# Ranking the experts on the chip and giving ScalarE and VectorE 64 slots for experts with few tokens, in a two-layer GLA/SSD trunk with a top-2-of-8 mixture of experts

## The chip, the cores and the metric

The kernel runs on one core of one Trainium2 chip. The metric is the device time of one execution in microseconds (us), and the time of a kernel is the median of several executions. Engines are named as the profile names them: PE (TensorE matmul), PEld (TensorE weight load), DVE (VectorE), ACT (ScalarE), POOL (GpSimd), SP (SyncE, which here issues the DMAs of the weights).

## The reference

Two layers work on 256 tokens of width 1024. Each layer is a mixer (gated linear attention beside a Mamba-2 scan) and a feed-forward part; the first layer has a dense SwiGLU, the second a mixture of 8 experts, of which each token uses 2:

```python
D_MODEL = 1024; SEQ = 256; D_FF = 3584; N_EXPERTS = 8; TOP_K = 2

def swiglu(t, w_gate, w_up, w_down):
    return (jax.nn.silu(t @ w_gate) * (t @ w_up)) @ w_down

def moe_swiglu(h, router_w, w_gate, w_up, w_down):
    t = h.reshape(bsz * seq, d)
    logits = (t @ router_w).astype(jnp.float32)
    top_v, top_i = lax.top_k(logits, TOP_K)
    top_p = jax.nn.softmax(top_v, axis=-1)
    gates = jnp.sum(jax.nn.one_hot(top_i, N_EXPERTS) * top_p[..., None], axis=1)
    out = jnp.zeros_like(t)
    for e in range(N_EXPERTS):
        out = out + gates[:, e:e + 1] * swiglu(t, w_gate[e], w_up[e], w_down[e])
    return out.reshape(bsz, seq, d)
```

256 tokens with 2 experts each make 512 pairs, 64 per expert on average. All data is float32.

## The kernel before

**Items.** The change touches the mixture of experts, which is the last and longest stage. The weights of an expert (3 matrices of 1024 x 3584) are cut into 42 pieces of 1 MiB, called items here. `moe_order` yields them: the hidden width is cut into 7 chunks `c` of 512, and each chunk has two items of gate weights (G), two of up weights (U) and two of down weights (D, one chunk behind). `moe_items` puts them on a plan, in the order of the experts 0 to 7.

**From memory to PE.** `pump` lets SP issue the DMA of the next planned item (L154) as soon as one of the staging buffers (`raw` twice, `xm`, `xx`, `q`, `xce`, `ada`, and `acc` in the first expert) is free. `split_whole` turns an item into two float32r halves, since PE multiplies in that format: ACT copies the high half (L182, 128x2048) and DVE subtracts it from the item (L183, 128x2048), after which the staging buffer is free. The halves go to `ws` slots, ten in all and two per item, and PE frees them.

**Slots.** Of the tokens an expert gets at most 128 at a time; `slot_map` (L1498) builds the matrix that gathers them, `gather` (L1512) gathers, and `split_cols` (L482, L495, L496) cuts the gathered tokens into high and low halves. `few` says of each expert whether it has at most 64 tokens. `is_narrow` (L1600) loads that into a register of PE, and `modal` (L1195) makes PE branch on it. With at most 64 tokens, high and low half of a token stand side by side as 128 columns, and an item costs PE 8 matmuls of 512 columns in place of 12 (`mm_slots`, L1205 and L1211 in place of L1207, L1208 and L1211); `folded` (L1256) then adds the two halves of each result, in place of a plain transpose (L1258). An expert with at most 64 tokens is called narrow below, another one wide.

**A chunk on ACT and DVE.** When gate and up products of a chunk are done, `run_experts` queues five steps, some items apart: `copy` (ACT, L1247, `gs` and `us`), `gate` (fold on PE, then SiLU on ACT, L1271), `hidden` (fold on PE, then a product on DVE, L1275), and `parted` (ACT copy L1280 and DVE subtraction L1281, which make the halves `fth` that the down product uses). All of these work on 128x512, that is 4 blocks of 128 slots, whether the expert is narrow or wide. Each engine works in the order in which its instructions are written.

**The next expert.** `at` places the rest by expert, chunk and item: at chunk 3 the slot map of the next expert, at chunk 4 its gather and split, and in chunks 1 and 2 the `combine` (L1560) of the expert before, which adds its output to `acc`. `make_gates` runs in expert 0, chunk 1.

Of the kernel before, what the change touches and what calls it, by code (L numbers as in the profile page):

```python
# [50 lines left out]
def trunk(ctx: ExitStack, tc: tile.TileContext, a: dict, out: bass.AP):  # L51
# [79 lines left out]
    def pump():  # L131
        n = len(raws)
        while n < len(extra) and state["dma"] < len(plan):
# [8 lines left out]
            elif kind == "adah":  # L142
                l, j, hf, k = what
                c0 = j * D + hf * 512
                view = a["ada_w"][l, k * 512:(k + 1) * 512, c0:c0 + 512].rearrange("(k p) n -> p k n", p=P)
            else:
                view = what
# [1090 lines left out]
    def run_experts(mo, experts, operand, fold, at):  # L1238
# [11 lines left out]
        def folded(src, narrow, p):  # L1250

            def body(nar):
                for k in range(4):
                    ks = slice(k * P, (k + 1) * P)
                    if nar:
                        pe.matmul(p[:, ks], src[:, ks], fold, start=True, stop=True)  # L1256
                    else:
                        pe.transpose(p[:, ks], src[:, ks], ident)  # L1258

            modal(narrow, body)  # L1260
            return p
# [7 lines left out]
        def gate(key):  # L1269
            sil[key] = mo.tile([P, FC], F, name=nm("fsg"), tag="fsg")  # L1270
            act.activation(sil[key], folded(gs.pop(key), ops[key[0]][1], ps_t()), AF.Silu)  # L1271

        def hidden(key):
            p, s = folded(us.pop(key), ops[key[0]][1], ps_mm()), sil[key]
            dve.tensor_tensor(s, p, s, op=OP.mult)  # L1275

        def parted(key):
            t = th[key] = mo.tile([P, 4, P, 2], R, name=nm("fth"), tag="fth", bufs=2)
            sv = sil.pop(key).rearrange("p (k t) -> p k t", k=4)
            act.activation(t[:, :, :, 0], sv, AF.Copy)  # L1280
            dve.tensor_tensor(t[:, :, :, 1], sv, t[:, :, :, 0].bitcast(F), op=OP.subtract)  # L1281

        for n, (kind, e, c, i) in enumerate(order):
# [3 lines left out]
            X, narrow = ops[e]  # L1287
# [58 lines left out]
    def moe_items(experts):  # L1346
        wg, wu, wd = a["moe_w_gate"][0], a["moe_w_up"][0], a["moe_w_down"][0]
        for kind, e, c, i in moe_order(experts):
            f0 = c * FC
            if kind in "GU":  # L1350
                w = (wg if kind == "G" else wu)[e, i * 512:(i + 1) * 512, f0:f0 + FC]
                w_item(w.rearrange("(k p) n -> p k n", p=P), [4, FC])
            elif kind == "D":
                w_item(wd[e, f0 + i * 256:f0 + (i + 1) * 256, :].rearrange("(k p) n -> p k n", p=P), [2, D])
            else:
                w_item(wd[e, f0:f0 + FC, i * 512:(i + 1) * 512].rearrange("(k p) n -> p k n", p=P), [4, 512])


    def moe(mo, ys, row, mT):
# [30 lines left out]
        few = mo.tile([P, NE], I32, name="few")  # L1390

# [98 lines left out]

        def slot_map(e, base):

            pm = pm_
            if base:
                sl = mo.tile([P, 2], F, name=nm("sl"), tag="sl", bufs=2)
                dve.tensor_scalar(sl, pos[:, :, e], float(-base), None, op0=OP.add)
            for t in range(2):
                dve.tensor_scalar(pm[:, t], iota_s, sl[:, t:t + 1] if base else pos[:, t, e:e + 1], mr[:, t, e:e + 1],  # L1498
# [3 lines left out]
        def pairs(e):  # L1502

            for t in range(2):
                dve.tensor_scalar(pm2[:, t], iota_h, pos[:, t, e:e + 1], mr[:, t, e:e + 1], op0=OP.is_equal, op1=OP.mult)
# [41 lines left out]
        def combine(e, pT, yhl, hf, first, dst, ps=ps_mm):  # L1547
            hs = slice(hf * 512, (hf + 1) * 512)
            for t in range(2):
# [6 lines left out]
                g = gates[:, t, e:e + 1]  # L1556
# [42 lines left out]
        def is_narrow(e):  # L1599
            return pe.value_load(few[0:1, e:e + 1], min_val=0, max_val=1)  # L1600
# [7 lines left out]

        def at(e, c, t, ys):
            nonlocal acc, fnw  # L1610
            where = (c, t)
            if e == 0:
                if where == (0, 1):
                    pT[0] = slots_T(0, pm, free, narrow[0])
                if where == (1, 1):
                    make_gates()
                if where == (0, 3):
# [14 lines left out]
            if e < NE - 1:  # L1632
# [4 lines left out]
                if where == (4, 1):  # L1637
                    split_cols(*gathered(e + 1, 0), *gather(m["pm"], 0, free))
                if where == (4, 3):
                    pT[e + 1] = slots_T(e + 1, m["pm"], free, narrow[e + 1])  # L1640
                if where == (4, 5):
                    split_cols(*gathered(e + 1, 1), *gather(m["pm"], 1, free))
# [12 lines left out]
        y = run_experts(mo, list(range(NE)), lambda e: (xg[e % 2], narrow[e]), fold, at)  # L1655
# [12 lines left out]
        with tc.If(over > 0):  # L1668
            xg.clear()
# [140 lines left out]
```

## Time and profile before

| | |
|---|---|
| median of three executions | 1522.16 us (1520.71 to 1522.85) |
| the profiled execution | 1522.08 us, its span 1520.3 us |
| first matmul of expert 0 | 570.0 us into the span |
| last matmul of the last expert | about 1508 us into the span |
| DVE, PE, ACT busy share of the span | 86%, 92%, 70% |
| read from memory | 480 MB, of it 352 MB for the experts |

The profile's span is 1.8 us shorter than the execution's own time, because some work lies around it. A busy share is an average over stages of different kinds; the stage of the experts has to be read alone, and there expert by expert. [...] The DMA share is the time of all packets over that of 16 engines, and can pass 1.

### The profile page before, as it was taken

The page shows a single profiled execution, that of the slowest core. Times are in us where ns is not written, and L with a number is a line of the kernel's source. Part 1 is how long each engine was busy: PE and PEld are TensorE (multiplying, and loading weights), DVE is VectorE, ACT ScalarE, POOL GpSimd, SP SyncE. Part 2 cuts the span into 40 slices and gives each one's busy share as a digit, 9 for nine tenths or more (in the row PEclk, how much of TensorE's full clock was granted, in tenths as well). Part 3 has the DMA queues.
Part 4 walks back from the last instruction along what each step waited for, and adds up shares of the span by engine and source line. Part 5 has one row for each costly group of instructions (what it writes and reads, how often), then busy time and mean ns, then how long its engine had stood idle before and what let it go on. Part 6 is the DMA issues. An engine that isn't in the chain of part 4 may idle for free.

```text
span 1520.3 us, 20693 instructions
## 1 busy us (share of the span) xinstructions
PE 1406.2 (92%) x7578; PEld 1203.3 (79%) x7578; DVE 1309.5 (86%) x1170; ACT 1069.5 (70%) x1258; POOL 41.5 (3%) x68
## 2 busy tenths in 40 slices
PE   4998899999999896999999899999899999999986
PEld 3886699999889785878888777777778888888764
DVE  7888878777757658999889999999999888888996
ACT  3474545444548457898778889898887777778875
POOL 2011000000010100000000000000000000000001
PEclk9999999999999988999999999999999999999988
DMA  9974688888844445999999999999999999999992
GB/s 335 311 249 158 230 279 318 314 321 308 298 148 146 140 165 205 380 379 398 375 320 371 389 398 402 404 402 402 406 403 400 381 325 351 346 321 376 384 375 96
DMA packets 204603, 483.15 MB, mean 318 GB/s; under 512 B 13119, under 2 KB 15405, under 8 KB 204462
## 3 DMA queue, kind: packets, MB, share of 16 engines
q1 hardware_dynamic: 203890, 480.05, 85.9%
q8 instruction: 98, 1.61, 0.4%
q10 hardware_dynamic: 428, 0.63, 0.1%
q0 software_dynamic: 144, 0.52, 0.1%
q14 instruction: 43, 0.35, 0.1%
HBM read 480.12 MB, written 1.05 MB: 316 GB/s over the span
## 4 chain that ended last, share of the span: by engine, by line
PE 44%; DVE 7%; issue 4%; ACT 4%; DMA 2%; POOL 0%; DVEq 0%; ACTq 0%
PE mm L1211 9%; DVE ws L183 5%; PE y L1211 5%; PE mm L1207 5%; PE mm L1208 5%; PE mm L1205 4%; PE y L1205 3%; PE y L1207 3%; PE y L1208 3%; ACT ws L182 2%; PE pt L1256 2%; PE y L1512 1%; PE mm L1256 1%; DMA raw<-in_moe_w_down 1%; DMA xm<-in_moe_w_down 1%
## 5 line engine op out<-in xcount | busy, mean ns | idle before, releaser
L174 ACT ACTIVATE ws<-raw 128x1024 fp32r<-128x1024 f32 x136 | 143.8, 1061 | 136.9 <-PE mm L428 64.1
L183 DVE TENSOR_TENSOR ws<-raw,ws 128x2048 fp32r<-128x2048 f32 x97 | 221.5, 2285 | 18.7 <-ACT ws L182 17.8
L175 DVE TENSOR_TENSOR ws<-raw,ws 128x1024 fp32r<-128x1024 f32 x136 | 164.3, 1221 | 56.5 <-ACT ws L174 55.9
L182 ACT ACTIVATE ws<-raw 128x2048 fp32r<-128x2048 f32 x97 | 185.8, 1916 | 32.0 <-PE y L1208 9.4
L1211 PE MATMUL y<-ws,fth 128*128 128x512 f32 x448 | 126.1, 404 | 0.0
L1211 PE MATMUL mm<-ws,hTh 128*128 128x512 f32 x448 | 122.1, 395 | 0.0
L1211 PE MATMUL mm<-ws,hTl 128*128 128x512 f32 x448 | 121.7, 393 | 0.0
L365 DVE SCALAR_TENSOR_TENSOR ada<-raw,s_col,ada 128x1024 f32<-128x1024 f32 (+1 forms) x98 | 114.3, 1167 | 2.1
L183 DVE TENSOR_TENSOR ws<-xx,ws 128x2048 fp32r<-128x2048 f32 x47 | 107.4, 2285 | 7.5 <-ACT ws L182 7.3
L183 DVE TENSOR_TENSOR ws<-ada,ws 128x2048 fp32r<-128x2048 f32 x47 | 107.4, 2285 | 7.3 <-ACT ws L182 7.3
L183 DVE TENSOR_TENSOR ws<-xm,ws 128x2048 fp32r<-128x2048 f32 x46 | 105.2, 2287 | 9.6 <-ACT ws L182 9.5
L183 DVE TENSOR_TENSOR ws<-xce,ws 128x2048 fp32r<-128x2048 f32 x47 | 107.3, 2284 | 6.8 <-ACT ws L182 6.8
L183 DVE TENSOR_TENSOR ws<-q,ws 128x2048 fp32r<-128x2048 f32 x47 | 107.3, 2284 | 5.4 <-ACT ws L182 4.8
L426 PE MATMUL mm<-hTh,ws 128*128 128x256 f32 x384 | 107.9, 281 | 0.0
L427 PE MATMUL mm<-hTh,ws 128*128 128x256 f32 x384 | 106.8, 278 | 0.0
L428 PE MATMUL mm<-hTl,ws 128*128 128x256 f32 x384 | 106.7, 278 | 0.0
L1211 PEld LDWEIGHTS y<-ws,fth 128*128 128x128 f32 x448 | 89.1, 199 | 19.9
L182 ACT ACTIVATE ws<-q 128x2048 fp32r<-128x2048 f32 x47 | 90.1, 1918 | 15.2 <-PE mm L1208 5.0
L182 ACT ACTIVATE ws<-ada 128x2048 fp32r<-128x2048 f32 x47 | 90.2, 1918 | 14.5 <-PE mm L1208 5.7
L1211 PEld LDWEIGHTS mm<-ws,hTh 128*128 128x128 f32 x448 | 85.5, 191 | 18.7
L1211 PEld LDWEIGHTS mm<-ws,hTl 128*128 128x128 f32 x448 | 85.8, 191 | 18.0
L182 ACT ACTIVATE ws<-xce 128x2048 fp32r<-128x2048 f32 x47 | 90.3, 1922 | 12.2 <-PE mm L1208 6.6
(378 smaller groups left out, 3451.1 us busy)
## 6 DMA issues: line engine op xcount, KB each, us to landing
raw<-in_ada_w SPq DMA_DIRECT2D x48, 1024.0 KB, 6.0
raw<-in_moe_w_up SPq DMA_DIRECT2D x33, 1024.0 KB, 6.6
raw<-in_moe_w_gate SPq DMA_DIRECT2D x32, 1024.0 KB, 7.8
raw<-in_moe_w_down SPq DMA_DIRECT2D x32, 1024.0 KB, 8.9
raw<-in_w_in SPq DMA_DIRECT2D x21, 1024.0 KB, 5.3
ada<-in_moe_w_down SPq DMA_DIRECT2D x17, 1024.0 KB, 8.8
xx<-in_moe_w_gate SPq DMA_DIRECT2D x16, 1024.0 KB, 7.5
q<-in_moe_w_gate SPq DMA_DIRECT2D x16, 1024.0 KB, 7.5
```

Of the source, the lines that this page charges most:

```text
L174: act.activation(h, src, AF.Copy)
L175: dve.tensor_tensor(lo, src, h.bitcast(F), op=OP.subtract)
L182: act.activation(h, r, AF.Copy)
L183: low = lambda: dve.tensor_tensor(lo, r, h.bitcast(F), op=OP.subtract)
L365: dve.scalar_tensor_tensor(acc, w, s_col[:, k:k + 1], acc, op0=OP.mult, op1=OP.add)
L426: pe.matmul(ps, xh, wh, start=start, stop=False)
L427: pe.matmul(ps, xl, wh, start=False, stop=False)
L428: pe.matmul(ps, xh, wl, start=False, stop=stop)
L1205: pe.matmul(ps, xs[:, 0:HALF].rearrange("p s two -> p (s two)"), wh, start=start, stop=False)
L1207: pe.matmul(ps, xs[:, :, 0], wh, start=start, stop=False)
L1208: pe.matmul(ps, xs[:, :, 1], wh, start=False, stop=False)
L1211: pe.matmul(ps, both if nar else xs[:, :, 0], wl, start=False, stop=stop)
```

## The change

The first expert stays expert 0. For the other seven the chip computes a rank by token count, and works on them in turns: the one with the most tokens, the one with the fewest, the second most, the second fewest and so on. The rank is made in expert 0 at chunk 1, item 3 (`arrange`, 18 instructions on DVE), and `order` then holds each expert's columns in the new order. SP loads the seven numbers into registers, and the DMAs of experts 1 to 7 take the expert from the register, which adds one register instruction to each of 294 DMAs. `is_narrow` loads its flag into registers of PE, ACT and DVE, and `modal` now also encloses the steps of ACT and DVE: in a narrow expert SiLU, `hidden`, `parted` and `split_cols` work on 4 blocks of 64 slots in place of 128.

```diff
+        def blocks(t, nar):
+            return t.rearrange("p (k t) -> p k t", k=4)[:, :, :HALF if nar else P]
...
         def hidden(key):
-            p, s = folded(us.pop(key), ops[key[0]][1], ps_mm()), sil[key]
-            dve.tensor_tensor(s, p, s, op=OP.mult)
+            src, p, s = us.pop(key), ps_mm(), sil[key]
+
+            def body(nar):
+                folded(src, nar, p)
+                sv = blocks(s, nar)
+                dve.tensor_tensor(sv, blocks(p, nar), sv, op=OP.mult)
+
+            modal(ops[key[0]][2], body)
...
+            def body(nar):
+                sv, tv = blocks(s, nar), t[:, :, :HALF if nar else P]
+                act.activation(tv[:, :, :, 0], sv, AF.Copy)
+                dve.tensor_tensor(tv[:, :, :, 1], sv, tv[:, :, :, 0].bitcast(F), op=OP.subtract)
...
+            def view():
+                return w[bass.ds(index(e), 1), r, n].rearrange("o (k p) n -> p (o k) n", p=P)
...
+        def arrange():
...
+            dve.scalar_tensor_tensor(key, cnt, float(NE), iota_e, op0=OP.mult, op1=OP.add)
+            dve.memset(key[:, 0:1], -1.0)
+            dve.tensor_tensor(pick, key[:, None, :].to_broadcast([P, NE, NE]),
+                              key[:, :, None].to_broadcast([P, NE, NE]), op=OP.is_lt)
+            dve.tensor_reduce(key, pick, axis=AX.X, op=OP.add)
...
+            dve.tensor_tensor(picked, pick[:, None].to_broadcast([P, 8, NE, NE]),
+                              info[:, :, None, :].to_broadcast([P, 8, NE, NE]), op=OP.mult)
+            dve.tensor_reduce(order, picked, axis=AX.X, op=OP.add)
...
         def is_narrow(e):
-            return pe.value_load(few[0:1, e:e + 1], min_val=0, max_val=1)
+            f = ids[0:1, 0, e:e + 1] if e else few[0:1, 0:1]
+            return pe.value_load(f, min_val=0, max_val=1), nc.values_load(
+                f, engines=[mybir.EngineType.PE, mybir.EngineType.Activation, mybir.EngineType.DVE], min_val=0, max_val=1)
...
+                if where == (1, 3):
+                    arrange()
+                    arranged[0] = True
+                    for i in range(1, NE):
+                        place[i] = sp.value_load(ids[0:1, 1, i:i + 1], min_val=0, max_val=NE - 1)
...
-                    split_cols(*gathered(e + 1, 0), *gather(m["pm"], 0, free))
+                    split_slots(e + 1, 0)
```

On DVE, in the middle of expert 2, a chunk's two own steps stand between the subtractions L183 of the items. Before:

```order
L183 TENSOR_TENSOR ws_8989<-xce_8748,ws_8988 128x2048
L1195 UNCONDITIONAL_BRANCH x2
L1275 TENSOR_TENSOR fsg_8921<-mm_8994,fsg_8921 128x512
L495 CAST hTl_5976<-sct_9014 128x512
L496 TENSOR_TENSOR hTl_5976<-sct_9014,hTl_5976 128x512
L183 TENSOR_TENSOR ws_9044<-raw_1169_8775,ws_9043 128x2048
L1195 UNCONDITIONAL_BRANCH
L1281 TENSOR_TENSOR fth_9049<-fsg_8921,fth_9049 128x512
L183 TENSOR_TENSOR ws_9074<-ada_8814,ws_9073 128x2048
```

The same two steps on DVE in the changed kernel, `hidden` (now L1285) and `parted` (now L1296), one chunk earlier, where no split of the next expert falls between them:

```order
L183 TENSOR_TENSOR ws_8803<-ada_8564,ws_8802 128x2048
L1195 COMPARE_AND_BRANCH
L1285 TENSOR_TENSOR fsg_8742<-mm_8808,fsg_8742 128x4x64
L1195 UNCONDITIONAL_BRANCH
L1285 TENSOR_TENSOR fsg_8742<-mm_8808,fsg_8742 128x512
L1195 UNCONDITIONAL_BRANCH x2
L183 TENSOR_TENSOR ws_8843<-raw_1120_8599,ws_8842 128x2048
L1195 COMPARE_AND_BRANCH
L1296 TENSOR_TENSOR fth_8848<-fsg_8742,fth_8848 128x4x64
L1195 UNCONDITIONAL_BRANCH
L1296 TENSOR_TENSOR fth_8848<-fsg_8742,fth_8848 128x512
L1195 UNCONDITIONAL_BRANCH x4
```

Each step stands twice, with 4x64 and with 512 elements, behind a compare-and-branch; one of the two is executed. The order of the long subtractions around them is the same. The steps of ACT changed in the same way.

On SP the register loads stand in the first expert, between the DMA of one staging buffer and that of the next. These are the last of the seven loads and what follows them:

```order
L1195 UNCONDITIONAL_BRANCH x2
L1700 TENSOR_LOAD ids
L1700 ISA x2
L154 DMA xx_5582<-in_moe_w_down 128x2x1024
L154 DMA q_723_5609<-in_moe_w_gate 128x4x512
L1195 UNCONDITIONAL_BRANCH x3
L154 DMA xce_5649<-in_moe_w_gate 128x4x512
```

The DMA into `xx` now stands behind all seven loads; before, it stood right behind the DMA into `xm`, which is the one ahead of the first load.

## Rows read from the trace of the kernel before

**Rows 1.** Windows between first `combine` of experts 1 to 7: length, busy, clock, DMA, GB/s.

```profile
716.28:841.06 124.78, 124.78 (x596) 105.11 (x595) 110.78 (x73) 100.50 (x82) 0.00 (x0) 1.00 0.98 358
841.06:949.66 108.60, 99.03 (x487) 81.80 (x486) 108.38 (x72) 93.53 (x81) 0.00 (x0) 0.97 1.03 398
949.66:1058.27 108.61, 101.36 (x498) 84.27 (x497) 108.38 (x72) 95.13 (x81) 0.00 (x0) 0.97 1.04 403
1058.27:1168.94 110.67, 103.98 (x498) 86.37 (x498) 108.67 (x73) 93.94 (x80) 0.00 (x0) 0.97 1.04 403
1168.94:1298.40 129.46, 129.46 (x604) 108.80 (x603) 111.38 (x72) 98.60 (x81) 0.00 (x0) 1.00 0.98 357
1298.40:1423.20 124.80, 124.80 (x596) 105.09 (x595) 110.77 (x73) 100.51 (x82) 0.76 (x1) 1.00 0.97 350
```

**Rows 2.** Timeline of DVE in a narrow expert: start, us, line, names, shapes.

```profile
1030.38 0.68 DVE L1275 TENSOR_TENSOR fsg<-mm,fsg 128x512 f32<-128x512 f32 x1
1030.98 2.28 DVE L183 TENSOR_TENSOR ws<-q,ws 128x2048 fp32r<-128x2048 f32 x1
1033.18 0.68 DVE L1281 TENSOR_TENSOR fth<-fsg,fth 128x512 fp32r<-128x512 f32 x1
1033.78 2.28 DVE L183 TENSOR_TENSOR ws<-xce,ws 128x2048 fp32r<-128x2048 f32 x1
```

**Rows 3.** Groups by form, expert 4 (974.5 to 1082.1): count, busy, mean ns, idle before.

```profile
L1280 ACT ACTIVATE fth<-fsg 128x512 fp32r<-128x512 f32 x7 | 4.8, 680 | 11.8 <-DVE fsg L1275 11.8
L182 ACT ACTIVATE ws<-xm 128x2048 fp32r<-128x2048 f32 x6 | 11.5, 1923 | 0.6 <-DMA xm<-in_moe_w_down 0.6
```

**Rows 4.** Groups of the whole span: DVE operations at 1024 and 256 elements.

```profile
L175 DVE TENSOR_TENSOR ws<-raw,ws 128x1024 fp32r<-128x1024 f32 x136 | 164.3, 1221 | 56.5 <-ACT ws L174 55.9
...
L692 DVE SCALAR_TENSOR_TENSOR xce<-xm,pcol,xce 128x256 f32<-128x256 f32 x36 | 16.9, 483 | 1.1 <-ACT xce L690 0.2
```

**Rows 5.** DMA issues and median us to landing, 770 to 800 us (expert 1).

```profile
q<-in_moe_w_down SPq DMA_DIRECT2D x2, 1024.0 KB, 6.0
```

**Rows 6.** The same view, 860 to 890 us (expert 2).

```profile
raw<-in_moe_w_gate SPq DMA_DIRECT2D x2, 1024.0 KB, 9.1
```

**Rows 7.** The same view, 1040 to 1070 us (expert 4).

```profile
xm<-in_moe_w_down SPq DMA_DIRECT2D x1, 1024.0 KB, 12.8
```

**Rows 8.** Timelines of DVE, SP and ACT in expert 0, where `arrange` will stand.

```profile
597.61 0.16 DVE L1470 TENSOR_REDUCE cmx<-cnt 128x1 f32<-128x8 f32 x1
...
597.87 0.22 DVE L1473 TENSOR_TENSOR pr<-mx 128x1 f32<-128x1 f32 x2
...
602.97 2.29 DVE L183 TENSOR_TENSOR ws<-xm,ws 128x2048 fp32r<-128x2048 f32 x1
606.86 2.29 DVE L183 TENSOR_TENSOR ws<-xx,ws 128x2048 fp32r<-128x2048 f32 x1 [1.60 <-ACT ws L182]
...
609.18 0.37 SPq L154 DMA_DIRECT2D xx<-in_moe_w_down  x1
...
623.70 1.91 ACT L182 ACTIVATE ws<-xx 128x2048 fp32r<-128x2048 f32 x1
```

**Rows 9.** Branches and register loads: duration ns min/median/max, first and last start.

```profile
L1195 PEldq COMPARE_BRANCH  x741: 63/176/406, 566.3 to 1501.6; - x186
...
L1668 PEldq COMPARE_BRANCH  x1: 3745/3745/3745, 1507.2 to 1507.2; - x1
L1668 DVEq COMPARE_BRANCH  x1: 72/72/72, 1511.3 to 1511.3; - x1
...
L1667 DVEq TENSOR_LOAD <-cmi x1: 546/546/546, 1510.7 to 1510.7; - x1
L1667 SPq TENSOR_LOAD <-cmi x1: 704/704/704, 1512.2 to 1512.2; - x1
```

**Rows 10.** Timeline of DVE at the end of the span.

```profile
1510.29 0.68 DVE L1582 TENSOR_TENSOR xm<-acc,hTh 128x512 f32<-128x512 f32 x1
1510.89 0.75 DVE L1587 TENSOR_SCALAR xm<-xm,fr 128x1024 f32<-128x1024 f32 x1
```

More of the change, by code (lines that the diff above doesn't have):

```diff
@@ L146, in pump @@
             else:
-                view = what
+                view = what() if callable(what) else what
             taken[i] = next(g for g in free_order(extra) if g not in [taken[k] for k in raws])
@@ L1248, in copied, with folded @@
             return out
[L1250 to L1260, printed above, removed]
-            return p
+        def folded(src, nar, p):
+            for k in range(4):
+                ks = slice(k * P, (k + 1) * P)
+                if nar:
+                    pe.matmul(p[:, ks], src[:, ks], fold, start=True, stop=True)
+                else:
+                    pe.transpose(p[:, ks], src[:, ks], ident)
+            return p
+        def blocks(t, nar):
+            return t.rearrange("p (k t) -> p k t", k=4)[:, :, :HALF if nar else P]
         def put(n, f, *args):
@@ L1286, in run_experts @@
                 ops[e] = operand(e)
-            X, narrow = ops[e]
+            X, narrow, _ = ops[e]
             if kind in "GU" and not i:
@@ L1390, in moe @@
         few = mo.tile([P, NE], I32, name="few")
+        turns = mo.tile([P, 4, 2], F, name="turns")
+        pool.iota(turns[:, :, 0], pattern=[[1, 4]], base=0, channel_multiplier=0, allow_small_or_imprecise_dtypes=True)
+        pool.iota(turns[:, :, 1], pattern=[[-1, 4]], base=7, channel_multiplier=0, allow_small_or_imprecise_dtypes=True)
+        key = mo.tile([P, NE], F, name="key")
+        pick = mo.tile([P, NE, NE], F, name="pick")
+        info = mo.tile([P, 8, NE], F, name="info")
+        order = mo.tile([P, 8, NE], F, name="order")
+        ids = mo.tile([P, 2, NE], I32, name="ids")
         lend(*MOE_TAGS)
@@ L1555, in combine @@
                     pe.matmul(p, pT[:, t].bitcast(F), yhl[0], start=True, stop=True)
-                g = gates[:, t, e:e + 1]
+                g = columns(e)[2][:, t:t + 1]
                 if first:
@@ L1607, in free, with split_slots, body @@
             return ps_y(1 - turn[0])
+        def split_slots(e, hf):
+            dst, (src, scale, shift) = gathered(e, hf), gather(m["pm"], hf, free)
+            def body(nar):
+                w = HALF if nar else P
+                split_cols(*[d[:, :, :w] for d in dst], src[:, :, :w], scale, shift)
+            modal(narrow[e][1], body)
         def at(e, c, t, ys):
@@ L1654, in moe @@
         acc = fnw = None
-        y = run_experts(mo, list(range(NE)), lambda e: (xg[e % 2], narrow[e]), fold, at)
+        y = run_experts(mo, list(range(NE)), lambda e: (xg[e % 2],) + narrow[e], fold, at)
         extra.remove("xm")
@@ L1669, in moe @@
             xg.clear()
+            arranged[0] = False
             for e in range(NE):
@@ L1747, in trunk @@
     mixer_items(1)
-    moe_items(range(NE))
+    place = {0: 0}
+    moe_items(range(NE), lambda i: place[i])
     pump()
```

60 lines of the change are left out of this document (42 added, 18 removed).

## The prediction

> **What bounds the kernel now.** The busy shares of the whole span say little, so I cut the stage of the experts at a fixed point of each expert's code, the first `combine` on DVE, and read the windows between these points [rows 1]. The number of PE instructions tells the kinds apart: about 490 in an interval that is mostly a narrow expert, about 600 in one that is mostly a wide one. With N for narrow and W for wide the order of the eight experts is N W N N N W W N, and the six windows are the steps WN, NN, NN, NW, WW, WN. In the step WW (129.46 us) PE is busy for all of it, and DVE for 111.38. In the steps NN (108.60 and 108.61 us) DVE is busy for 108.38 us, and PE has gaps. So a wide expert is bound by PE and a narrow one by DVE.
>
> The DMA share and GB/s of the same windows show a third resource. A wide step moves 357 GB/s at a share of 0.98, a narrow one 403 at 1.04, and 403 is also the most that the following step reaches. I take 403 GB/s as about what the DMAs give, though nothing in the trace proves that they can do no more. The time from issue to landing says how near this is: 6.0 us in the first wide expert [rows 5], 9.1 us in the narrow one after it [rows 6], 12.8 us in the third narrow one in a row [rows 7]. Only there ACT begins to wait for the data, by 0.6 us for one buffer [rows 3]. So staged data covers about 12.8 - 6.0 = 6.8 us of extra waiting, and a run of narrow experts uses it up.
>
> **The change part by part.** The sum is made against the profiled execution's own 1522.08 us, which lies within 0.1 us of the median of 1522.16.
>
> *The turns.* With five narrow and three wide experts, and expert 0 narrow, the new order is N W N W N W N N. Between the same cuts that gives three steps WN, two NW and one NN in place of two WN, one NW, two NN and one WW; the first step (NW, from expert 0 to the first wide one) is there in both. The new steps cost 3 x 124.79 + 2 x 110.67 + 108.6 = 704.3 us against 706.9 before [rows 1]: **-2.6 us**. It is small because a step costs nearly the same whatever stands beside it.
>
> *Half width on DVE.* A chunk's two own steps take DVE 0.60 us each from start to start (1030.38 to 1030.98, 1033.18 to 1033.78), without a gap around them [rows 2]. For half the elements I take the slope of DVE: 1.221 us for 1024 elements [rows 4] against 0.68 us for 512 [rows 2], 0.54 us for 512 more, so 0.27 us for 256. The only row at 256 elements, another operation, takes 0.483 us [rows 4], which would leave 0.20. I take 0.27, since it is the same operation. A narrow expert has 14 such steps, 3.7 us, and the five have **-18.7 us**; with 0.20 it is -14. `split_cols` for a narrow expert also gets shorter, but runs in the expert ahead of it, which is wide in three of four cases and waits for PE: nothing.
>
> *Half width on ACT.* ACT waits 11.8 us per narrow expert for DVE's product `hidden` [rows 3], so what it saves becomes more of this waiting: nothing. The cover is DVE; if DVE stopped being the bound, ACT would be next with some 94 us of work per narrow step [rows 1], too far off to matter.
>
> *`arrange`.* Of its 18 instructions on DVE, eight copies of 8 elements cost about 0.11 us (two independent ones took 0.22), eight dependent small ones 0.16 to 0.2 [rows 8], and the two on 512 elements 0.6 [rows 2]: about 3.5 us. It stands where DVE sat idle for 1.60 us before the subtraction of `xx` [rows 8]. That leaves **+1.9 us**; 0 if DVE's next gaps in that expert swallow the rest, 3.5 if none of it is hidden.
>
> *SP.* The seven loads hold up the DMA into `xx` and all behind it. A load took 0.70 us on SP [rows 9] with some 0.2 around it, so 6.4 us at most, beginning when `arrange` ends; the DMA would have waited for the subtraction of `xx` (2.2 us) in any case, so it is at most some 4 us late. Before, 14.5 us passed from its issue at 609.18 to its use at 623.70 [rows 8], and landing takes about 6 us there, as in [rows 5]. The 8 us between cover it: nothing, 4 us if a full queue shortens that cover. The added register instruction of each DMA runs on SP, which waits for buffers: nothing.
>
> *Branches.* DVE and ACT now run 182 compare-and-branches each, and a jump at the end of each narrow body. On DVE the one in the trace took 0.072 us, on PE the 741 took 0.063 to 0.406 us [rows 9]. What decides is whether the sequencer does this while the engine works. One row speaks for it: the sequencer of DVE began a register load at 1510.7 [rows 9], while DVE worked on the instruction that began at 1510.29 and ahead of the start of the next at 1510.89 [rows 10], and that next one followed without a gap. Ahead of nearly every branch stands a subtraction of 2.2 us. So I take **0**. No row shows a branch on DVE between two long operations, so the price stays open: from 0 up to the full 0.063 + 0.176 us for each of 23 branches with their jumps in a narrow expert, 5.5 us per expert. A gain has no mechanism here.
>
> [...]
>
> *The DMAs.* A faster narrow expert asks for more: 44.0 MB in 108.6 - 3.7 = 104.9 us are 420 GB/s, and at 403 they take 109.3 us. So a narrow expert outruns the DMAs by 4.4 us. Beside that, landing got 3 us longer in the first narrow expert even at its present pace [rows 5, 6]. The 6.8 us of cover are thus just used up by a narrow expert that follows a wide one: I charge 0.6 us for each of three. A wide expert restores the cover, since it leaves 129.46 - 109.3 = 20 us. The last expert follows a narrow one, finds no cover, and its loads end 7 items ahead of its end: 4.4 x 35/42 = 3.7 us. Together **+5.5 us**; 0 if the DMAs can do 420 GB/s.
>
> The sum is -2.6 - 18.7 + 1.9 + 5.5 = -13.9 us, so 1522.1 - 13.9 = 1508.2, and I say **1508 us**. Its own range is 1500 (DMAs no limit, `arrange` hidden) to 1515 (0.20 us per step, SP's delay felt).
>
> **The rivals.**
>
> *The DMAs are the bound of every narrow expert.* For it speaks that landing times rose through all three narrow experts in a row [rows 6, 7]: even the present pace is more than the DMAs sustain. If the cover is gone early in each expert, narrow experts 3, 5, 7 and 8 of the new order keep their 108.6 us, and only expert 0 gains. Then the sum is -2.6 - 3.7 + 1.9, and the time 1517.7. Against it speaks that ACT waited for data only in the third.
>
> *Branches cost DVE.* If DVE's sequencer doesn't run ahead over a branch, each of the 115 branches of the narrow experts, with its jump, stops DVE for 0.14 us (DVE's own 0.072 twice) to 0.24 us. That is 16 to 28 us in the stretches where DVE is the bound, and the time 1524 to 1536; I say 1530. From 0.12 us per pair the gain is gone, from 0.15 us the kernel is slower by over 0.2%. For it: no branch of the trace stands in a busy stretch of ACT or DVE. Against it: [rows 10].
>
> *Code that isn't there.* The last branch of PE, which leaps over a long piece of code, took 3.745 us [rows 9], while the 741 that skip a few instructions stayed under 0.41. If some of DVE's short skips behaved like the long one, six of them would eat the gain, and ten in narrow experts would give 1508 + 37 = 1545. [...]
>
> *No change.* Exposed branches at 0.1 us a pair, or the DMA limit together with a felt `arrange`, leave 1519 to 1525; I say 1521.
>
> **How the numbers follow.** The forecast has a chance of 0.57, the DMA bound 0.16, no change 0.10, branches on DVE 0.13, code fetch 0.04. This kernel's measurement can tell about 0.2%, 3 us, from no change. The forecast and the DMA rival are faster by more than that: 0.73. No change has 0.10, and slower is the sum of the last two, 0.17. For 8 in 10 the range must reach through the DMA rival and no change, and leaves out the slower ones: 1499 to 1523, with the low end where the sum has neither DMA limit nor `arrange` and the turns are worth a little more.
>
> **What would show it.** Right: steps NN and WN of the new trace about 3 us shorter than [rows 1], DVE still busy for nearly all of a narrow stretch, `hidden` and `parted` at about 0.42 us (0.33 us from start to start), landing times that climb to 12 us within each narrow expert and fall to 6 in each wide one. The DMA rival would show narrow steps of 108 us or more, with DVE idle behind ACT and ACT behind DMAs. Branches would show as gaps of 0.1 us or more on DVE beside L1285 and L1296, with nothing that ended them. The prediction is wrong if the wide experts get longer than 129.5 us, since nothing here touches PE's work in them.

## The result, and the profile after

| | before | changed |
|---|---|---|
| median | 1522.51 us (4 runs, 1520.71 to 1524.62) | **1504.33 us** (4 runs, 1503.49 to 1504.58) |
| profiled execution, its span | 1522.08, 1520.3 us | 1503.49, 1501.7 us |

The ratio is 0.9879, with a 95% interval of 0.9862 to 0.9896: faster by 18 us. The forecast was 1508 with a range of 1499 to 1523.

The windows between the first `combine` (now L1628, for the first one L1626) of one expert and the next, in the order N W N W N W N N, in the columns of [rows 1]: length, busy time and instructions of PE, PEld, DVE, ACT and POOL, granted clock, DMA share, GB/s.

```profile
714.46:838.29 123.83, 123.83 (x592) 104.69 (x592) 109.10 (x73) 98.95 (x82) 0.00 (x0) 1.00 0.99 361
838.29:946.52 108.23, 103.82 (x502) 86.05 (x502) 105.61 (x72) 90.76 (x80) 0.00 (x0) 0.98 1.04 402
946.52:1070.38 123.86, 123.86 (x592) 104.74 (x592) 109.11 (x73) 98.97 (x82) 0.00 (x0) 1.00 0.99 363
1070.38:1178.59 108.21, 103.81 (x502) 86.00 (x502) 105.57 (x72) 90.73 (x80) 0.00 (x0) 0.98 1.04 402
1178.59:1302.42 123.83, 123.83 (x592) 104.70 (x592) 109.08 (x72) 98.89 (x82) 0.00 (x0) 1.00 0.99 361
1302.42:1409.60 107.18, 98.98 (x490) 81.04 (x489) 104.26 (x73) 91.18 (x80) 0.74 (x1) 0.98 1.04 403
```

The steps that are mostly wide stay bound by PE (busy for all of 123.83 us). The narrow ones got shorter, from 108.6 or 110.67 us to 107.2 or 108.2, and DVE's busy time fell from 108.4 to 104.3 in the step NN. The same two steps of a chunk on DVE that [rows 2] shows of before, in the last pair of narrow experts (start, us, names, shapes):

```profile
1303.74 2.28 DVE L183 TENSOR_TENSOR ws<-raw,ws 128x2048 fp32r<-128x2048 f32 x1
1305.94 0.41 DVE L1285 TENSOR_TENSOR fsg<-mm,fsg 128x256 f32<-128x256 f32 x1
1306.28 2.28 DVE L183 TENSOR_TENSOR ws<-xm,ws 128x2048 fp32r<-128x2048 f32 x1
1308.48 0.42 DVE L1296 TENSOR_TENSOR fth<-fsg,fth 128x256 fp32r<-128x256 f32 x1
1308.81 2.28 DVE L183 TENSOR_TENSOR ws<-xx,ws 128x2048 fp32r<-128x2048 f32 x1
```

Each now takes 0.34 us from start to start (1305.94 to 1306.28) in place of 0.60, and the next subtraction follows without a gap, although a branch stands on each side.

Cut at five points of the code, the 18.6 us between the two spans lie here. `make_gates` is taken at its first instruction on DVE that writes `gates`, the last `combine` at its start.

| stretch | before | changed | difference | forecast |
|---|---|---|---|---|
| start to `make_gates` in expert 0 | 598.84 | 597.32 | -1.5 | 0 |
| `make_gates` to first `combine` of expert 1 | 117.44 | 117.14 | -0.3 | -1.8 |
| six steps to the first `combine` of the last expert | 706.92 | 695.14 | -11.8 | -12.1, with the next |
| from there to the last `combine` | 82.79 | 79.38 | -3.4 | |
| last `combine` to the end | 14.3 | 12.7 | -1.6 | 0 |

The first row can't be put down to the change: in the ten kernels profiled for this study that point lies anywhere from 596.7 to 601.5 us, and in the one with the least edit, a single added load, at 596.67. So kernels are compared below from `make_gates` on.

One more thing has to be known before steps are compared. At the end of a narrow expert with a wide one behind it, called a seam below, PE waits some 2 us for ACT's `gs` and is then busy without a gap. At some seams the granted clock, PE's as a share of full speed, falls there from 1.00 to 0.50 (at the first seam of the changed kernel from 674.2 to 677.6 us, for 3.4 us), at others it stays at 1.00. Two seams of one kernel, branch_only (it is described below), show both: 12 us around each seam in the columns of [rows 1], and PE's first instruction behind the wait.

```profile
909.66:921.66 12.00, 9.61 (x43) 7.79 (x42) 12.00 (x8) 11.05 (x9) 0.00 (x0) 0.86 1.04 411
1144.81:1156.81 12.00, 9.66 (x50) 7.95 (x50) 12.00 (x8) 11.06 (x10) 0.00 (x0) 1.00 1.04 410
```

```profile
913.60 1.16 PE L1255 MATMUL pt<-fold,gs 128*128 128x128 f32 x8 [2.39 <-ACT gs L1247]
1148.75 1.16 PE L1255 MATMUL pt<-fold,gs 128*128 128x128 f32 x8 [2.34 <-ACT gs L1247]
```

PE is busy for as long in both, and gets 43 matmuls done in place of 50. The step NW with the fall takes 110.69 us, the one without it 109.14. dve_half has such a pair too, 109.00 us (0.86) and 107.42 (1.00). So I estimate the price of a fall at a seam as 1.6 us. No run changed the clock by itself, and why it falls at one seam and not at another stays open, since the wait ahead is nearly the same. In the kernel before, the clock falls at one of its two seams (from expert 4 to 5, but not from 0 to 1), in the changed kernel at all three.

### The profile page after: what moved, and what is told of

Its sections match the earlier page's. It is cut to its first block, busy times and chain, and to the rows that moved or that the text cites. A ratio compares the mean times of both kernels' runs of the same rounds, so it can differ in the third digit from the quotient of the medians.

```text
span 1501.7 us, 22118 instructions
## 1 busy us (share of the span) xinstructions
PE 1402.7 (93%) x7578; PEld 1199.4 (80%) x7578; DVE 1290.1 (86%) x1187; ACT 1053.6 (70%) x1258; POOL 41.1 (3%) x70
## 5 line engine op out<-in xcount | busy, mean ns | idle before, releaser
L183 DVE TENSOR_TENSOR ws<-raw,ws 128x2048 fp32r<-128x2048 f32 x97 | 221.7, 2287 | 21.1 <-ACT ws L182 20.8
L1207 PE MATMUL mm<-ws,hTl 128*128 128x512 f32 x336 | 134.9, 402 | 0.0
L1208 PE MATMUL mm<-ws,hTl 128*128 128x512 f32 x336 | 132.5, 394 | 0.0
L1205 PE MATMUL mm<-ws,hTh 128*128 128x512 f32 x448 | 125.3, 402 | 2.8 <-ACT hTh L506 2.2
L1211 PE MATMUL mm<-ws,hTl 128*128 128x512 f32 x448 | 122.1, 394 | 0.0
L1211 PE MATMUL mm<-ws,hTh 128*128 128x512 f32 x448 | 122.0, 394 | 0.0
L183 DVE TENSOR_TENSOR ws<-xm,ws 128x2048 fp32r<-128x2048 f32 x46 | 105.2, 2288 | 11.3 <-ACT ws L182 11.3
L183 DVE TENSOR_TENSOR ws<-ada,ws 128x2048 fp32r<-128x2048 f32 x47 | 107.5, 2288 | 7.9 <-ACT ws L182 7.9
L183 DVE TENSOR_TENSOR ws<-xce,ws 128x2048 fp32r<-128x2048 f32 x47 | 107.5, 2287 | 7.5 <-ACT ws L182 7.5
L183 DVE TENSOR_TENSOR ws<-xx,ws 128x2048 fp32r<-128x2048 f32 x47 | 107.4, 2286 | 6.2 <-ACT ws L182 6.1
L183 DVE TENSOR_TENSOR ws<-q,ws 128x2048 fp32r<-128x2048 f32 x47 | 107.5, 2286 | 4.8 <-ACT ws L182 4.3
```

The costliest lines, as they stand in the source:

```text
L183: low = lambda: dve.tensor_tensor(lo, r, h.bitcast(F), op=OP.subtract)
L1205: pe.matmul(ps, xs[:, 0:HALF].rearrange("p s two -> p (s two)"), wh, start=start, stop=False)
L1207: pe.matmul(ps, xs[:, :, 0], wh, start=start, stop=False)
L1208: pe.matmul(ps, xs[:, :, 1], wh, start=False, stop=False)
L1211: pe.matmul(ps, both if nar else xs[:, :, 0], wl, start=False, stop=stop)
```

## The experiments

Eight kernels ran, each against the kernel before on the same chip. The last five columns come from the profiled execution, four of them in us; the last one counts the seams at which the clock fell.

| kernel | median | ratio to before, 95% | `make_gates` to first `combine` | six steps | last expert | end | falls |
|---|---|---|---|---|---|---|---|
| before | | | 117.44 | 706.92 | 82.79 | 14.3 | 1 of 2 |
| changed | 1504.33 | 0.9879 (0.9862 to 0.9896) | 117.14 | 695.14 | 79.38 | 12.7 | 3 of 3 |
| turns_only | 1518.41 | 0.9971 (0.9960 to 0.9982) | 119.93 | 703.39 | 82.83 | 12.2 | 3 of 3 |
| half_only | 1514.19 | 0.9941 (0.9927 to 0.9955) | 116.46 | 701.91 | 79.31 | 14.2 | 1 of 2 |
| branch_only | 1517.36 | 0.9966 (0.9955 to 0.9977) | 119.95 | 701.84 | 82.81 | 11.8 | 2 of 3 |
| dve_half | 1506.02 | 0.9891 (0.9874 to 0.9908) | 116.57 | 695.10 | 80.74 | 12.5 | 1 of 3 |
| rank_idle | 1521.23 | 0.9983 (0.9973 to 0.9994) | 119.92 | 704.17 | 82.80 | 12.0 | 1 of 2 |
| rev_turns | 1502.50 | 0.9866 (0.9848 to 0.9885) | 113.21 | 697.24 | 79.32 | 12.8 | 2 of 3 |
| all_narrow | 1468.75 | one execution | 113.18 | 663.47 | 80.13 | 12.7 | no seam |
| sp_load | 1519.98 | 0.9993 (0.9984 to 1.0002) | 117.45 | 706.95 | 82.82 | 13.0 | 1 of 2 |

### The two parts apart: turns_only and half_only

turns_only keeps the ranking and the order, and leaves the steps of ACT and DVE at full width, outside the branches, as in the kernel before:

```diff
         def is_narrow(e):
             f = ids[0:1, 0, e:e + 1] if e else few[0:1, 0:1]
-            return pe.value_load(f, min_val=0, max_val=1), nc.values_load(
-                f, engines=[mybir.EngineType.PE, mybir.EngineType.Activation, mybir.EngineType.DVE], min_val=0, max_val=1)
+            return (pe.value_load(f, min_val=0, max_val=1),)
```

> The turns alone: the rank, the register loads and the new order stay, but SiLU, hidden, parted and split work on 128 slots without a branch on ScalarE and VectorE, as before. Theory (a narrow expert is bound by VectorE, a wide one by TensorE, and steps add up): -2.6 us from the steps and +1.8 us for the rank, so 1521.5 us, no change that can be told. Rival (the mix of the two kinds is what gains, because staged data smooths it): a good part of the measured 18 us, below 1514 us.

The windows of its steps WN and NW:

```profile
718.47:842.93 124.46, 124.46 (x595) 105.18 (x595) 110.76 (x72) 100.45 (x82) 0.00 (x0) 1.00 0.98 353
842.93:953.62 110.69, 104.45 (x500) 87.00 (x499) 108.67 (x72) 92.75 (x80) 0.00 (x0) 0.97 1.04 399
```

Each is within 0.4 us of the same kind of step in [rows 1], so the order alone changes little, as the forecast had it. The time fell by 4.5 us, where no change that can be told was expected: beside the steps (-3.5 us) the end got 2.1 us shorter, which no term had. The rival, below 1514 us, falls.

half_only keeps the branches and the half width, and works on the experts in the order 0 to 7 without a ranking:

```diff
-                return w[bass.ds(index(e), 1), r, n].rearrange("o (k p) n -> p (o k) n", p=P)
+                return w[e, r, n].rearrange("(k p) n -> p k n", p=P)
...
-                if where == (1, 3):
-                    arrange()
...
-    moe_items(range(NE), lambda i: place[i])
+    moe_items(range(NE))
```

> The half width alone: experts in the order 0 to 7 (N W N N N W W N), no rank, static addresses, branches on ScalarE and VectorE as in the changed kernel. Theory with a DMA ceiling at 403 GB/s: the first narrow expert of the run of three gains its 3.7 us from the cover, the other two are held near 108 us, experts 0 and 7 gain 3.7 us each, so about -12 us, 1510 us, and ScalarE waits for DMAs by several us in experts 3 and 4. Rival without a ceiling: all five gain, -18.7 us, 1503.5 us, and the turns were worth nothing.

The turns alone give 0.3%, the half width alone 0.6%, together 1.2%: 4.5 and 8.7 us are 5 us less than the two give together. In the profiled executions 3.2 us of this lie in the six steps (-3.5 and -5.0 apart, -11.8 together), and 1.8 us in the stretch ahead of them (+2.5 and -1.0 apart, -0.3 together). The 1.8 us are about one fall of the clock: at the first seam, from expert 0 to 1, it falls in turns_only, in half_only and in the changed kernel, but not in the kernel before, so its price stands in both parts and only once in the whole. Where the steps lose is seen in the windows of half_only, the steps WN, NN, NN and NW:

```profile
717.32:841.15 123.83, 123.83 (x592) 104.68 (x592) 109.10 (x73) 98.94 (x82) 0.00 (x0) 1.00 0.98 355
841.15:946.62 105.47, 98.94 (x490) 81.39 (x490) 104.07 (x72) 90.18 (x80) 0.00 (x0) 0.98 1.04 403
946.62:1057.18 110.56, 101.66 (x499) 82.50 (x498) 105.25 (x72) 94.61 (x81) 0.00 (x0) 0.98 1.04 403
1057.18:1167.68 110.50, 103.42 (x505) 84.43 (x504) 106.13 (x72) 94.96 (x81) 0.00 (x0) 1.00 1.04 403
```

The first narrow step gains 3.1 us against [rows 1] and DVE is busy for nearly all of it. The second is 2 us longer than before the change, with DVE busy for only 105.25 of 110.56 us and the DMAs at 403 GB/s in both. The issue and landing of DMAs at 1040 to 1070 us of half_only (count, KB, median us), and what DVE and ACT wait for from 946.62 to 1167.68 (waiter, releaser: us in total, times, longest):

```profile
ada<-in_moe_w_down SPq DMA_DIRECT2D x2, 1024.0 KB, 13.7
```

```profile
DVE ws L183 <- ACT ws L182: 7.8, 19, 1.2
...
ACT ws L182 <- DMA q<-in_moe_w_down: 2.9, 4, 0.8
ACT ws L182 <- DMA ada<-in_moe_w_down: 2.5, 4, 0.7
```

DVE waits for ACT, and ACT for data, in row after row (twelve more of ACT's rows name a DMA). So three narrow experts in a row outrun the DMAs, and the wide expert between them is what lets the half width through. The theory of a ceiling holds, but its 1510 us was 4 us too low, since the second and third step took 110.5 us and not about 108. The rival without a ceiling, 1503.5 us, falls.

### The ceiling by itself: all_narrow

Every expert is taken as narrow. The tokens beyond 64 of the three wide ones are left out, so this kernel computes less, and only its steps are read.

```diff
-        dve.tensor_scalar(few, pp[:, 16:24], float(HALF), None, op0=OP.is_le)
+        dve.tensor_scalar(few, pp[:, 16:24], float(2 * P), None, op0=OP.is_le)
...
-            dve.tensor_scalar(ids[:, 0], order[:, 6], float(HALF), None, op0=OP.is_le)
+            dve.tensor_scalar(ids[:, 0], order[:, 6], float(2 * P), None, op0=OP.is_le)
```

> The flags of all experts are forced to narrow, everything else as in the changed kernel; the tokens beyond 64 of the three wide experts are left out of the sum. Eight narrow experts in a row show the steady step. DMA-bound theory: the first steps 105 to 107 us, then 109 to 110.5 us each at 398 to 403 GB/s, landing at 13 to 14 us and VectorE idle 4 to 6 us per step. Rival, VectorE is the bound and the DMAs can do 420 GB/s: all steps 105 us, landing at about 10 us. The span is then about 1460 by the first and 1430 by the second.

Three of the six windows, and the waits of DVE and ACT from 932.52 to 1152.73:

```profile
932.52:1042.59 110.07, 101.00 (x497) 82.27 (x496) 105.03 (x72) 93.99 (x81) 0.00 (x0) 0.98 1.04 401
1042.59:1152.73 110.14, 101.78 (x492) 82.57 (x492) 104.99 (x72) 93.86 (x81) 0.00 (x0) 0.97 1.04 402
1152.73:1262.85 110.12, 99.39 (x485) 81.15 (x484) 104.93 (x73) 94.21 (x81) 0.00 (x0) 0.97 1.04 401
```

```profile
DVE ws L183 <- ACT ws L182: 9.4, 22, 1.7
...
ACT ws L182 <- DMA raw<-in_moe_w_down: 3.2, 5, 0.7
ACT ws L182 <- DMA raw<-in_moe_w_up: 3.0, 4, 0.8
```

The steps settle at 110.1 us, and none was at 105. DVE has 105.0 us of work in each and idles for 5.1. The steps of 105 to 107 us that were expected first did not come: the first window took 111.55 us, and landing was at 14 to 15 us just ahead of it (700 to 730 us). An expert's 44.04 MB in 110.1 us are 400 GB/s, and landing stayed at 12 to 15 us. This is as close to a price of the disputed resource as these runs come: a narrow expert at half width is 5.1 us too fast for the DMAs. The forecast had 4.4.

### The branches: branch_only

The flags go to ACT and DVE, and every branch is executed as in the changed kernel, but both bodies work at full width:

```diff
         def blocks(t, nar):
-            return t.rearrange("p (k t) -> p k t", k=4)[:, :, :HALF if nar else P]
+            return t.rearrange("p (k t) -> p k t", k=4)[:, :, :P]
...
-                w = HALF if nar else P
+                w = P
```

(and the same in `parted`.)

> The changed kernel with all its branches, register loads and turns, but both bodies of a branch work on 128 slots. Beside turns_only it has the 182 branches on ScalarE and on VectorE and nothing else. Theory (the sequencer runs ahead while the engine works): within 1 us of turns_only. Rival (a branch stops VectorE for 0.05 to 0.14 us with its jump, 115 of them where VectorE is the bound): 6 to 16 us above turns_only.

Branches of L1195 in branch_only: duration in ns, min/median/max.

```profile
L1195 PEldq COMPARE_BRANCH  x854: 63/176/416, 567.3 to 1499.6; - x171
L1195 ACTq COMPARE_BRANCH  x295: 34/38/50, 589.0 to 1497.5; - x148
L1195 DVEq COMPARE_BRANCH  x295: 43/47/63, 590.0 to 1498.2; - x148
```

DVE executes 295 branches, the 182 that the prediction counted and 113 jumps behind the narrow bodies, 13.9 us of its sequencer's time at 47 ns. Against turns_only, which has none on DVE or ACT, the stretches from `make_gates` to the last `combine` are the same to 0.02 us, but for one step that is 1.56 us shorter (109.14 against 110.70). That is the step whose seam has no fall of the clock, shown above; in turns_only the clock falls at all three. So the branches cost nothing that these runs can tell.

### Only DVE at half width: dve_half

```diff
             def body(nar):
                 folded(src, nar, p)
-                act.activation(blocks(s, nar), blocks(p, nar), AF.Silu)
+                act.activation(blocks(s, False), blocks(p, False), AF.Silu)
...
-                act.activation(tv[:, :, :, 0], sv, AF.Copy)
+                act.activation(t[:, :, :, 0], blocks(s, False), AF.Copy)
```

> The changed kernel with SiLU and the copy of parted on ScalarE at 128 slots again (split stays at 64): only VectorE has the half width in a chunk's own steps. Theory (ScalarE waits for VectorE in narrow experts): the time of the changed kernel, 1504.3 us, within 1 us; ScalarE's wait for hidden falls from 10.7 us to some 8 us. Rival (the chain hidden, parted's copy, next item's copy on ScalarE paces VectorE): 2 to 3 us longer.

The six steps take 695.10 us, as in the changed kernel, but the equal sum hides unequal steps. Where the clock falls at the seam in both kernels, the step is 0.8 us longer (109.00 against 108.23); where it falls only in the changed kernel, 0.8 us shorter (107.42 against 108.21). The last expert is 1.4 us longer. From `make_gates` to the end dve_half takes 0.5 us longer; with 1.6 us for each of the two falls that it lacks, ACT's half width is worth 3 to 4 us, an estimate. The medians differ by 1.7 us, with intervals that overlap, so neither this nor the zero that was expected is shown. ACT's wait for `hidden` stayed at 10.4 us in the step NN, where some 8 was expected.

### What the ranking costs: rank_idle

Based on turns_only: the same instructions of `arrange`, loads and register DMAs, but the rank is made from the expert's number, so that the order stays 0 to 7:

```diff
-        pool.iota(turns[:, :, 0], pattern=[[1, 4]], base=0, channel_multiplier=0, allow_small_or_imprecise_dtypes=True)
-        pool.iota(turns[:, :, 1], pattern=[[-1, 4]], base=7, channel_multiplier=0, allow_small_or_imprecise_dtypes=True)
+        pool.iota(turns[:, :, 0], pattern=[[2, 4]], base=0, channel_multiplier=0, allow_small_or_imprecise_dtypes=True)
+        pool.iota(turns[:, :, 1], pattern=[[2, 4]], base=1, channel_multiplier=0, allow_small_or_imprecise_dtypes=True)
...
-            dve.scalar_tensor_tensor(key, cnt, float(NE), iota_e, op0=OP.mult, op1=OP.add)
+            dve.scalar_tensor_tensor(key, cnt, 0.0, iota_e, op0=OP.mult, op1=OP.add)
```

> The ranking and SP's loads are made as in the changed kernel, but the ranks come from the expert's number alone, so the experts stay in the order 0 to 7; ScalarE and VectorE keep full width. Theory: the six steps stay within 0.3 us of the kernel before (124.8, 108.6, 108.6, 110.7, 129.5, 124.8); the first combine of expert 1 comes 2 to 2.5 us later after make_gates (117.4 us before, 119.9 in turns_only), which is the price of the ranking in a DVE-bound expert; and the end after the last combine is 12.3 us in place of 14.3, because SP has loaded a register before. Together about 1522.5, the same as before. Rival 1: the shorter end belongs to the order of the experts, then it stays 14.3 us and the time is about 1525. Rival 2: the ranking costs nothing, then 1520.5.

The stretch from `make_gates` to the first `combine` is 2.5 us longer than before, the end 2.3 us shorter. Of the six steps, which were expected to stay, only two moved by over 0.4 us: the one with the two wide experts took 127.85 us in place of 129.46 (in half_only it was 127.72), that before it 110.26 in place of 110.67. Together they are 2.0 us shorter, and at the seam in them the clock falls in the kernel before (0.86 from 1124.27 to 1136.27) and stays at 1.00 here and in half_only. At the first seam it is the other way round; 12 us there, of before and then of rank_idle:

```profile
674.84:686.84 12.00, 9.72 (x50) 8.41 (x51) 12.00 (x7) 12.00 (x9) 0.00 (x0) 1.00 1.03 366
677.48:689.48 12.00, 9.64 (x44) 7.83 (x43) 12.00 (x8) 11.12 (x9) 0.00 (x0) 0.86 1.03 392
```

So some 1.7 of the 2.5 us (12 us at 0.86) are the clock, and the ranking itself costs about 0.8 us, an estimate. It agrees with the 0.7 us between half_only (116.46) and the changed kernel (117.14), which both have the fall there. The time is 0.2% under that of before. Rival 1 falls, since the end is short without the new order. Rival 2, a ranking that costs nothing, was nearer in the time (1520.5) and is off by this 0.8 us.

### Does the place of the pair matter: rev_turns

```diff
-        pool.iota(turns[:, :, 0], pattern=[[1, 4]], base=0, channel_multiplier=0, allow_small_or_imprecise_dtypes=True)
-        pool.iota(turns[:, :, 1], pattern=[[-1, 4]], base=7, channel_multiplier=0, allow_small_or_imprecise_dtypes=True)
+        pool.iota(turns[:, :, 0], pattern=[[-1, 4]], base=8, channel_multiplier=0, allow_small_or_imprecise_dtypes=True)
+        pool.iota(turns[:, :, 1], pattern=[[1, 4]], base=1, channel_multiplier=0, allow_small_or_imprecise_dtypes=True)
+        pool.memset(turns[:, 0, 0:1], 0.0)
```

> Turns the other way round: fewest, most, second fewest and so on, so N N W N W N W N; half width as in the changed kernel. Theory: a pair of narrow experts costs the same wherever it stands, since the second outruns the DMAs (landing climbs to 13 us and VectorE waits some 2 us); here the pair stands at the start of the stage, where landing is at 7.5 to 10.5 us already, so VectorE waits 2 us in expert 1, and the last expert, behind a wide one, has landings under 11 us and ends 2 us sooner. Time 1502 to 1506, same as the changed kernel's 1504. Rival: the loss belongs to the end of the stage, then this order gives 1501 or less.

The time is 1502.50 us; its interval overlaps that of the changed kernel, so it isn't shown to be better, and it reaches down to the rival's 1501. The waits of DVE and ACT in its second narrow expert (711.38 to 822.78):

```profile
DVE ws L183 <- ACT ws L182: 4.2, 11, 1.1
...
ACT ws L182 <- DMA raw<-in_moe_w_down: 2.4, 4, 0.7
ACT ws L182 <- DMA ada<-in_moe_w_up: 2.0, 2, 1.2
```

The waiting for data moved with the pair, as expected, and came to 4.2 us in place of the expected 2. But the last expert did not end sooner (79.32 against 79.38 us): its share of the loss had not been there. This speaks against the rival too, by which the loss belongs to the end of the stage.

### The end of the kernel: sp_load

The kernel before, with one register load on SP in expert 0 whose value nothing uses:

```diff
                 if where == (1, 1):
                     make_gates()
+                    sp.value_load(few[0:1, 0:1], min_val=0, max_val=1)
```

> The kernel before with one addition: in expert 0, behind make_gates, SP loads one flag into a register that nothing uses. Theory: the end of the kernel got shorter in every kernel with the ranking because SP had loaded a register before; then SP's register load at the end takes about 0.28 us in place of 0.70, its eight semaphore instructions begin 2.8 us behind its branch in place of 3.7, and the stretch after the last combine is about 12.3 us in place of 14.3. The six steps stay as before, and the time falls by 1 to 2 us, to some 1521. Rival: the shorter end comes with the DMAs that take the expert from a register; then it stays 14.3 us, and the time is that of before.

At the end each engine loads the flag of an overflow, and leaps over the code for it; then SP runs eight semaphore instructions. SP's rows of that, of before and then of sp_load (count, ns min/median/max, first and last start). SP's register load before is in [rows 9], 704 ns.

```profile
L1668 SPq EVENT_SEMAPHORE  x8: 17/17/17, 1517.0 to 1517.6; - x8
...
L1668 SPq COMPARE_BRANCH  x1: 50/50/50, 1513.3 to 1513.3; - x1
```

```profile
L1669 SPq EVENT_SEMAPHORE  x8: 17/17/17, 1513.4 to 1514.5; - x8
...
L1669 SPq COMPARE_BRANCH  x1: 50/50/50, 1510.6 to 1510.6; - x1
...
L1668 SPq TENSOR_LOAD <-cmi x1: 287/287/287, 1510.0 to 1510.0; - x1
```

The load falls from 704 to 287 ns, the way from branch to first semaphore from 3.7 to 2.8 us, and the end from 14.3 to 13.0 us, where 12.3 was expected. So most of the shorter end comes from SP having loaded a register before; the rest of it (11.8 to 12.8 us in kernels with the ranking) stays unexplained. In the time, 0.07%, it is not told from no change.

## Why the prediction was right, and where its steps were off

**What bounds what: right.** In the changed kernel the wide steps are PE's and the narrow ones DVE's (105.6 of 108.23 us). ACT still waits for DVE's product there, 11.3 us where [rows 3] had 11.8. That ACT's half width is worth nothing, as the forecast had it, isn't shown: dve_half lets it be 3 to 4 us.

**Half width on DVE: right in size.** 0.27 us was forecast for each step, and the timeline has 0.26 (0.60 less 0.34). (14 times 0.27 is 3.8 and not 3.7, which is too little to matter.) Taken from turns_only to the changed kernel, which have the same order and a fall at each seam, the gain of a narrow expert between two wide ones is 0.63 + 2.46 = 3.1 us, the forecast's 3.7 less its 0.6 for DMAs. But the 0.6 was right for a wrong reason. From 838.29 to 946.52 us ACT waits for no DMA at all; DVE's gaps lie at 916 to 945 us, where the wide expert begins, and stand behind ACT's waits for that expert's matmuls (L1208 is a wide expert's). ACT's first two rows in this window:

```profile
ACT fth L1295 <- DVE fsg L1285: 11.3, 6, 2.8
ACT ws L182 <- PE mm L1208: 3.5, 5, 1.3
```

So some of what DVE saves is kept by PE, at the seam to a wide expert. The same gaps, at 685 to 712 us, take part of expert 0's gain, which was 2.8 us (119.93 to 117.14).

**The DMAs: right mechanism, and the term that failed.** The forecast took the 6.8 us of cover as used up by the first narrow expert, and let the pair at the end lose 0.6 + 3.7 = 4.3 us of the 7.5 that half width saves it. From turns_only to the changed kernel the pair gained 0.62 + 1.43 + 3.45 = 5.5 us (its steps WN and NN and the last expert), so it lost 2.0. The cover lasts longer than the forecast had it. In half_only the first step NN takes 105.47 us, close to DVE's 104.9, although the expert is followed by more narrow ones. DMAs issued 20 to 50 us into that step landed after 8 to 9 us, those from 80 us on after 13 to 15, such as this one:

```profile
raw<-in_moe_w_down SPq DMA_DIRECT2D x1, 1024.0 KB, 14.8
```

In the changed kernel DVE waits in the last pair six times from 1377 to 1408 us, 2.4 us together. Here is the longest, and a DMA issued at 1380 to 1410 us:

```profile
1391.71 2.29 DVE L183 TENSOR_TENSOR ws<-raw,ws 128x2048 fp32r<-128x2048 f32 x1 [1.03 <-ACT ws L182]
```

```profile
raw<-in_moe_w_down SPq DMA_DIRECT2D x1, 1024.0 KB, 13.9
```

In the last expert, from 1409.6 us on, DVE's subtractions wait for ACT only 0.2 us in all. The sign that the forecast named for landing came true: about 5 us in the first wide expert (770 to 800 us), 9 and then up to 12 in the narrow one behind it. One reading of the forecast was short: beside the wait of 0.6 us for one buffer in [rows 3] the same view has 0.6 for `raw` and 0.4 for `ada`, 1.6 together. So of the 4.7 us by which the profiled execution beat the sum, the pair has 2.3, the end of the kernel 1.6, and the turns 0.9; the scatter at the start (1.5) and expert 0 (1.5 the other way) cancel.

**The turns: nearly right.** -2.6 us was forecast for the steps; turns_only has 703.39 us against 706.92, that is -3.5, because the steps WN got 0.3 us shorter too. But that the two lie near each other is in part luck. rank_idle has the ranking and the old order, and its steps take 704.17 us, only 0.8 us more than those of turns_only: its steps WN are 0.3 us shorter as well, and its one seam in these steps has no fall, where turns_only has two. The forecast took 110.67 us for a step NW, a row with a fall in it; without the fall it is 109.14. With half width beside them the turns are worth 6.8 us in the steps (701.91 to 695.14), 3.2 more than alone, since they keep narrow experts from standing in a row, and the forecast had this only as the difference between its sum and a rival.

**`arrange`: right in its own time, too high in its price.** Its instructions (17; the 18 of the text above is one too many) took 3.27 us on DVE, from 603.39 to 606.66, against 3.5. The forecast counted one idle time of 1.60 us as cover [rows 8] and left 1.9; a second one of 0.60 us behind it was also there in the kernel before. The measured price is 0.7 us at half width, where both kernels have the fall at the first seam, and 2.5 at full width, of which some 1.7 are the fall that only the kernel with the ranking has. So without the clock the price is 0.7 to 0.8 us, and the forecast's 1.9 was some 1 us too high. These are its first two instructions and its last, with the subtraction of `xx` right behind, without a gap:

```profile
603.39 0.17 DVE L1538 COPY info<-pos 128x8 f32<-128x8 f32 x1
603.46 0.17 DVE L1539 COPY info<-mr 128x8 f32<-128x8 f32 x1
...
606.59 0.17 DVE L1555 CAST ids<-order 128x8 int32<-128x8 f32 x1
606.66 2.29 DVE L183 TENSOR_TENSOR ws<-xx,ws 128x2048 fp32r<-128x2048 f32 x1
```

**SP: right.** The DMA into `xx` was issued 13.8 us behind `make_gates` (611.12) in place of 10.3 (609.18), so 3.5 us later, within the 4 us allowed, and no engine of the changed kernel waits for a DMA in the rest of expert 0.

**Branches: right.** branch_only puts them at 0 and ends the rival in which they cost DVE. One branch has a median of 47 ns on DVE, 38 on ACT and 176 on PE. DVE's sequencer does it while the engine works: in the changed kernel the subtraction at 1306.28 us follows a product of 0.41 us that began at 1305.94, with a branch between them and no gap. The rival "Code that isn't there" is ended too: the longest branch of L1195 on DVE took 63 ns, on ACT 50. Why the last branch of PE took 3.745 us, no run shows. (By the forecast's own figures four long ones, 4 x 3.745 = 15 us, would have eaten the gain, and not six.)

**The other rivals.** "The DMAs are the bound of every narrow expert" gave 1517.7 us. That is what the half width alone comes near to (1514.19), and it doesn't hold where a wide expert stands between. "No change" fell with the medians.

**Not in the sum at all:** the end of the kernel, 1.6 us shorter, and the clock at the seams. The changed kernel has falls at three seams in its profiled execution and the kernel before at one, by the estimate above some 3 us that the changed kernel pays on top; they are hidden in the measured prices of the turns and of `arrange`.

## What to carry to other kernels

Before an engine's work is made shorter, compute from bytes and the new time which rate it will ask for, and compare it with the rate at which the steady windows stop rising: here 420 GB/s was asked and 400 given. Then the order of light and heavy pieces is part of the optimization, since staged data covered the faster pace only for a while (in the first step NN of half_only landing rose from 8 to 9 us to 13 to 15 within some 80 us); parts measured alone (4.5 and 8.7 us) can add up to less than the whole (18 us). A branch that skips one or two instructions was free here, at 47 ns on DVE beside instructions of 0.4 to 2.3 us. And before a difference of 1 or 2 us between two profiles is put down to an edit, the granted clock of the stretch has to be compared: here one fall at a seam was as large as several of the terms.

## What the runs showed of the hardware that was not expected

The first register load on SP made a later part of the program faster: with one unused load in the middle, SP's load at the end took 287 ns in place of 704, and the way from its branch to its first semaphore 2.8 us in place of 3.7. Why the second of these shrinks the trace doesn't say.

Behind nearly the same wait of PE (2.39 and 2.34 us, for the same instruction of ACT) the granted clock had a mean of 0.86 over 12 us around one seam of branch_only and of 1.00 at another, and the steps differ by 1.55 us.

A start point that the change doesn't touch, `make_gates`, lay between 596.7 and 601.5 us in the profiled executions of the ten kernels, so a difference of two spans holds scatter of up to 4.8 us that belongs to earlier stages. Cuts at fixed points of the code agreed to 0.05 us between kernels that should agree there and whose clock falls at the same seams (117.44 and 117.45; 119.92, 119.93 and 119.95).
